# Interleaved rotary embedding on one core: sin products in free row places, whole-row VectorE instructions, and four transfers taken apart

## The chip, the cores and the metric

The kernel runs on one core of a Trainium2 chip. The metric is device time in microseconds of one execution, here the median of three runs. VectorE, GpSimd and 16 DMA engines do the work; ScalarE and SyncE issue one transfer each, TensorE has nothing to do.

## The reference

`x` is (8, 2048, 16, 64) in fp32: batch, sequence position, head, head dimension. `cos` and `sin` are (2048, 32). Neighbouring elements of the head dimension form pairs that are rotated by the angle of their position:

```
x1, x2 = x[..., 0::2], x[..., 1::2]
out[..., 0::2] = x1 * cos - x2 * sin
out[..., 1::2] = x1 * sin + x2 * cos
```

`cos` and `sin` hold for all batches and heads of a position. The output is fp32, of the shape of `x`.

## The kernel before, in words

The 2048 positions are split over 128 partitions, 16 positions (`K = 16`) to a partition, so that one batch element is one "row": 16 sub-rows of 1024 elements in each partition. A row is 8 MB in DRAM and 4 MB in SBUF, where it lies as bf16: the transfers of GpSimd's queue cast on the way in and on the way out. SBUF holds six row places (`buf`, shown as the tile `xt`); `at = [0, 1, 2, 3, 4, 5, 0, 1]` says which place row b uses, so rows 6 and 7 take the places of rows 0 and 1.

For each group of sub-rows `rotate` issues three VectorE instructions: the product with the sin table into `qt` (line 78), the product with the cos table in place (line 84), and the sum of the row with the pairs of `qt` exchanged (line 90). The sin table holds (sin, -sin) in turn, the cos table every value twice. Before, `qt` is one small buffer of its own of four sub-rows (`KP = 4`), and `rotate_row` goes through a row in four such groups, 12 instructions to a row.

The order is written out by hand (`tc.manual_schedule`); each engine works its own instructions in that order, with semaphores between them where data or places are shared.

- Start: ScalarE's queue loads the first four sub-rows of row 0 as fp32 into place 5, where `cos` and `sin` arrive as well; GpSimd's queue issues load(0) (the other 12 sub-rows), cos, sin, load(1) and load(2, 2), which is rows 2 and 3 in one transfer. VectorE casts the first sub-rows (line 107) and makes both tables (lines 109 to 114). Then place 5 is free and GpSimd issues load(4, 2).
- Middle: VectorE rotates rows 0 to 3. GpSimd waits to issue store(0, 2): in row 3's second group, after the first `GATE` sub-rows of the sin product, VectorE copies one element of place 0 onto itself (line 83, the gate), and the store waits for that copy. store(2, 2) follows when row 3 is done, then load(6, 2), which waits until stores 0 and 1 have landed, then store(4, 2) after row 5.
- End: store(6), then store(7) of 12 sub-rows. Before the last four sub-rows VectorE copies one element into row 6's place (line 140), and so waits until store(6) has landed; their sum goes as fp32 into place 3, and SyncE's queue stores it (line 142).

Transfers of GpSimd's queue are worked in the order of issue. `load` issues at line 56, `store` at line 59.

Of the kernel before, what the change touches and what calls it, by code (L numbers as in the profile page):

```python
# [2 lines left out]

# [4 lines left out]


@with_exitstack  # L10
def kernel(
    ctx: ExitStack,
    tc: tile.TileContext,
    x: bass.AP,
    cos: bass.AP,
    sin: bass.AP,
    out: bass.AP,
):
    nc = tc.nc
    fp32 = mybir.dt.float32  # L20
    bf16 = mybir.dt.bfloat16
    mult = mybir.AluOpType.mult
    add = mybir.AluOpType.add

    B, S, H, D = x.shape
    P = 128
    K = S // P
    D2 = D // 2
    HD = H * D
    NX = 6  # L30
    KP = 4
    HEAD = 4
    TAIL = 4
    GATE = 1

    x_t = x.rearrange("b (p k) h d -> p b k (h d)", p=P, k=K)
    out_t = out.rearrange("b (p k) h d -> p b k (h d)", p=P, k=K)
    cos_t = cos.rearrange("(p k) c -> p (k c)", p=P, k=K)
    sin_t = sin.rearrange("(p k) c -> p (k c)", p=P, k=K)

    consts = ctx.enter_context(tc.tile_pool(name="consts", bufs=1))
    rows_pool = ctx.enter_context(tc.tile_pool(name="rows", bufs=1))
    stage = ctx.enter_context(tc.tile_pool(name="stage", bufs=1))

    c_tab = consts.tile([P, K, D], bf16)
    s_tab = consts.tile([P, K, D], bf16)


    buf = rows_pool.tile([P, NX, K, HD], bf16, name="xt")
    at = [0, 1, 2, 3, 4, 5, 0, 1]  # L50

    def place(b, n=1, k0=0, k1=K):
        return buf[:, at[b] : at[b] + n, k0:k1]

    def load(b, n=1, k0=0, k1=K):
        nc.gpsimd.dma_start(out=place(b, n, k0, k1), in_=x_t[:, b : b + n, k0:k1])  # L56

    def store(b, n=1, k0=0, k1=K):
        nc.gpsimd.dma_start(out=out_t[:, b : b + n, k0:k1], in_=place(b, n, k0, k1))  # L59

    def rotate(b, k0=0, k1=K, gate=None, to=None):
        nk = k1 - k0
        xp = buf[:, at[b], k0:k1]
        qt = stage.tile([P, KP, HD], bf16, name="qt", tag="work")

        def rows(a):
            return a.rearrange("p k (h e) -> p k h e", h=H, e=D)

        def tab(a, j0=0, j1=nk):
            return dataclasses.replace(  # L70
                a,
                offset=a.offset + (k0 + j0) * D,
                ap=[a.ap[0], [D, j1 - j0], [0, H], [1, D]],
            )


        for a, z in ((0, nk),) if gate is None else ((0, GATE), (GATE, nk)):
            nc.vector.tensor_tensor(  # L78
                out=rows(qt[:, a:z]), in0=rows(xp[:, a:z]), in1=tab(s_tab, a, z), op=mult
            )  # L80
            if z < nk:
                one = buf[:1, at[gate], 0, :1]
                nc.vector.tensor_copy(out=one, in_=one)  # L83
        nc.vector.tensor_tensor(out=rows(xp), in0=rows(xp), in1=tab(c_tab), op=mult)  # L84
        q_swap = dataclasses.replace(
            qt, offset=qt.offset + 1, ap=[qt.ap[0], [2, nk * HD // 2], [-1, 2]]
        )
        x3 = xp.rearrange("p k (a j) -> p (k a) j", j=2)
        y3 = x3 if to is None else to.rearrange("p k (a j) -> p (k a) j", j=2)
        nc.vector.tensor_tensor(out=y3, in0=x3, in1=q_swap, op=add)  # L90

    with tc.manual_schedule():

        def fp32_in(b, k0, k1):
            return buf[:, at[b], k0:k1].rearrange("p k e -> p (k e)").bitcast(fp32)

        head = fp32_in(5, 0, 2 * HEAD).rearrange("p (k e) -> p k e", e=HD)
        cos_sb = fp32_in(5, K - 2, K - 1)
        sin_sb = fp32_in(5, K - 1, K)
        nc.scalar.dma_start(out=head, in_=x_t[:, 0, :HEAD])  # L100
        load(0, k0=HEAD)
        nc.gpsimd.dma_start(out=cos_sb, in_=cos_t)  # L102
        nc.gpsimd.dma_start(out=sin_sb, in_=sin_t)  # L103
        load(1)
        load(2, 2)

        nc.vector.tensor_copy(out=buf[:, at[0], :HEAD], in_=head)  # L107
        s2 = s_tab.rearrange("p k (i j) -> p (k i) j", j=2)
        nc.vector.tensor_copy(out=s2[:, :, 0], in_=sin_sb)  # L109
        nc.vector.tensor_scalar_mul(s2[:, :, 1], sin_sb, -1.0)  # L110
        nc.vector.tensor_copy(  # L111
            out=c_tab.rearrange("p k (i j) -> p (k i) j", j=2),
            in_=cos_sb.to_broadcast([P, K * D2, 2]),
        )

        load(4, 2)

        def rotate_row(b, k1=K, gate=None):
            for k in range(0, k1, KP):
                rotate(b, k, k + KP, gate if k == KP else None)  # L120

        rotate_row(0)
        rotate_row(1)
        rotate_row(2)
        rotate_row(3, gate=0)
        store(0, 2)
        store(2, 2)
        load(6, 2)
        rotate_row(4)
        rotate_row(5)  # L130
        store(4, 2)
        rotate_row(6)
        store(6)
        rotate_row(7, K - TAIL)
        store(7, k1=K - TAIL)

        tail = fp32_in(3, 0, 2 * TAIL).rearrange("p (k e) -> p k e", e=HD)
        nc.vector.tensor_copy(out=buf[:1, at[6], 0, :1], in_=buf[:1, at[7], K - 1, :1])  # L140
        rotate(7, K - TAIL, K, to=tail)
        nc.sync.dma_start(out=out_t[:, 7, K - TAIL :], in_=tail)


# [1 line left out]
_INS = ['x', 'cos', 'sin']  # L146
_OUTS = [((8, 2048, 16, 64), 'float32')]


# [23 lines left out]
```

## Time and profile before

| what | value |
|---|---|
| median of 3 runs | 316.95 us (316.95 to 317.0) |
| the profiled execution: own time, span | 316.72 us, 314.9 us |
| VectorE busy | 225.9 us (72%), 103 instructions |
| GpSimd busy | 7.9 us (2%), 16 instructions |
| HBM read, written | 67.63 MB, 67.11 MB |
| packets' time on GpSimd's queue (q0), share of 16 engines | 96.6% |

The profile is of one execution. Its span goes from the first to the last instruction; 1.8 us of the execution's time lie outside it. The page shows the span in 40 slices of 7.87 us. Its GB/s count what is written: 200 in a slice of loads (bf16) and 400 in a slice of stores (fp32) are the same traffic on the DRAM side. A group's row gives line, engine, operation, shapes and count, then busy time and the mean ns of one instruction, then the idle time ahead of it and what ended that. A row of a window gives its two ends, its length, the busy time of VectorE (DVE) and GpSimd (POOL) with instruction counts, the granted clock of TensorE, the DMA engines' busy share and GB/s.

### The profile page before, as it was taken

To read this page: it belongs to the slowest core of one execution; us is meant where nothing else is said; L and a number is where in the kernel's file an instruction comes from. 1 tells how busy PE (TensorE), PEld (TensorE's weight loads), DVE (VectorE), ACT (ScalarE), POOL (GpSimd) and SP (SyncE) were. 2 spreads that over 40 slices of the span, in tenths; PEclk is the share of its full clock that TensorE was granted. 3 is DMA by queue.
4 is the path that set the end of the run, shared out by engine and by line. 5 is a ranking of instruction groups with operands and counts; after the bars stand their busy time and mean duration, and the time that the engine had idled before them with its cause. 6 is when DMAs were issued, how large, how long until landed. Compare 5 with 4: busy or idle time off the path is not lost.

```text
span 314.9 us, 176 instructions
## 1 busy us (share of the span) xinstructions
DVE 225.9 (72%) x103; POOL 7.9 (2%) x16
## 2 busy tenths in 40 slices
DVE  0029999999899999999999995000009999992550
POOL 4000000000000000000000000000000000000000
DMA  7999999999999999999999999999999999999996
GB/s 255 261 283 200 200 208 258 200 200 221 246 200 200 246 221 400 400 516 417 400 400 524 408 400 400 262 204 200 204 320 408 400 449 474 408 400 483 425 424 266
DMA packets 2658, 102.25 MB, mean 325 GB/s; under 512 B 225, under 2 KB 225, under 8 KB 353
## 3 DMA queue, kind: packets, MB, share of 16 engines
q0 software_dynamic: 2368, 98.04, 96.6%
q10 hardware_dynamic: 144, 2.10, 1.8%
q1 hardware_dynamic: 144, 2.10, 1.6%
q14 instruction: 2, 0.01, 0.0%
HBM read 67.63 MB, written 67.11 MB: 428 GB/s over the span
## 4 chain that ended last, share of the span: by engine, by line
DVE 65%; DMA 16%; another core or an unknown queue 14%; issue 1%; POOL 0%; DVEq 0%; PEldq 0%
DVE xt L90 22%; DVE xt L84 21%; DVE qt L78 21%; DMA out_dram<-xt 9%; DMA xt<-in_sin_dram 7%; POOL xt L56 0%; DVE c_tab L111 0%; POOL xt L102 0%; DVE s_tab L109 0%; DVE s_tab L110 0%; DVE xt L140 0%; DVE xt L83 0%; DVEq L78 0%; PEldq L168 0%
## 5 line engine op out<-in xcount | busy, mean ns | idle before, releaser
L78 DVE TENSOR_TENSOR qt<-xt,s_tab 128x4096 bf16<-128x4096 bf16 (+2 forms) x33 | 73.4, 2226 | 45.1 <-DMA xt<-in_x_dram 44.2
L90 DVE TENSOR_TENSOR xt<-xt,qt 128x4096 bf16<-128x4096 bf16 (+1 forms) x32 | 75.5, 2359 | 1.1
L84 DVE TENSOR_TENSOR xt<-xt,c_tab 128x4096 bf16<-128x4096 bf16 x32 | 73.4, 2292 | 1.1
L107 DVE CAST xt<-xt 128x4096 bf16<-128x4096 f32 x1 | 2.3, 2294 | 15.3 <-DMA xt<-in_x_dram 15.3
L59 POOL DMA_DIRECT2D out_dram<-xt x5 | 3.2, 644 | 235.1 <-DVE xt L90 143.6
L140 DVE COPY xt<-xt 1x1 bf16<-1x1 bf16 x1 | 0.1, 144 | 9.1 <-DMA out_dram<-xt 9.1
L109 DVE CAST s_tab<-xt 128x512 bf16<-128x512 f32 x1 | 0.5, 452 | 6.3 <-DMA xt<-in_sin_dram 6.3
L56 POOL DMA_DIRECT2D xt<-in_x_dram x5 | 3.4, 683 | 43.3 <-DMA out_dram<-xt 21.3
L111 DVE CAST c_tab<-xt 128x1024 bf16<-128x1024 f32 x1 | 0.7, 684 | 0.0
L103 POOL DMA_DIRECT2D xt<-in_sin_dram x1 | 0.6, 562 | 0.0
L102 POOL DMA_DIRECT2D xt<-in_cos_dram x1 | 0.6, 554 | 0.0
L110 DVE TENSOR_SCALAR s_tab<-xt 128x512 bf16<-128x512 f32 x1 | 0.4, 442 | 0.0
L83 DVE COPY xt<-xt 1x1 bf16<-1x1 bf16 x1 | 0.1, 136 | 0.0
L157 POOL MEMSET const-float32-0.0<- 128x1 f32 x1 | 0.1, 98 | 0.2 <-issue 0.2
L157 POOL MEMSET const-bfloat16-1.0<- 128x1 bf16 x1 | 0.1, 101 | 0.0
L157 POOL MEMSET const-float32-1.0<- 128x1 f32 x1 | 0.1, 98 | 0.0
L157 POOL MEMSET const-uint8-127<- 128x1 uint8 x1 | 0.1, 98 | 0.0
## 6 DMA issues: line engine op xcount, KB each, us to landing
xt<-in_x_dram POOLq DMA_DIRECT2D x3, 8192.0 KB, 78.2
out_dram<-xt POOLq DMA_DIRECT2D x1, 6144.0 KB, 23.3
xt<-in_x_dram POOLq DMA_DIRECT2D x1, 4096.0 KB, 40.1
xt<-in_x_dram POOLq DMA_DIRECT2D x1, 3072.0 KB, 21.3
xt<-in_x_dram ACTq DMA_DIRECT2D x1, 2048.0 KB, 14.6
out_dram<-xt SPq DMA_DIRECT2D x1, 2048.0 KB, 10.2
xt<-in_cos_dram POOLq DMA_DIRECT2D x1, 256.0 KB, 21.3
xt<-in_sin_dram POOLq DMA_DIRECT2D x1, 256.0 KB, 21.4
```

The source lines that it names most:

```text
L56: nc.gpsimd.dma_start(out=place(b, n, k0, k1), in_=x_t[:, b : b + n, k0:k1])
L59: nc.gpsimd.dma_start(out=out_t[:, b : b + n, k0:k1], in_=place(b, n, k0, k1))
L78: nc.vector.tensor_tensor(out=rows(qt[:, a:z]), in0=rows(xp[:, a:z]), in1=tab(s_tab, a, z), op=mult)
L84: nc.vector.tensor_tensor(out=rows(xp), in0=rows(xp), in1=tab(c_tab), op=mult)
L90: nc.vector.tensor_tensor(out=y3, in0=x3, in1=q_swap, op=add)
L102: nc.gpsimd.dma_start(out=cos_sb, in_=cos_t)
L103: nc.gpsimd.dma_start(out=sin_sb, in_=sin_t)
L107: nc.vector.tensor_copy(out=buf[:, at[0], :HEAD], in_=head)
L109: nc.vector.tensor_copy(out=s2[:, :, 0], in_=sin_sb)
L110: nc.vector.tensor_scalar_mul(s2[:, :, 1], sin_sb, -1.0)
L111: nc.vector.tensor_copy(out=c_tab.rearrange("p k (i j) -> p (k i) j", j=2), in_=cos_sb.to_broadcast([P, K * D2, 2]),)
L157: nc = _bacc.Bacc("TRN2", target_bir_lowering=False, num_devices=1)
```

## The change

The buffer for the sin products shrinks in use: `rotate` gets `via`, the number of a row place that is free at that time, and writes its products there; without `via` it uses the small buffer, now allocated once. With `via` most rows are done whole:

- rows 0 and 1 whole, through place 4; load(4) is issued after row 1, so it waits for that row's last sum;
- the first half of row 2 in one group of eight sub-rows, through place 5; load(5) is issued after it; the rest of row 2 and all of row 3 stay in groups of four;
- the gate in row 3 stands after two sub-rows instead of one; store(0) and store(1) are issued one by one;
- rows 4 and 5 whole, through place 0, so row 4 waits until store(0) has landed; load(6, 2) comes after them and waits for row 5's last sum;
- row 6 whole and the first 12 sub-rows of row 7 in one group, through place 2; the last four through place 2 too.

GpSimd instead of VectorE makes the sin table, ahead of load(4) in its queue. VectorE has 61 instructions instead of 117 (waits and the like counted).

```diff
-    GATE = 1
+    GATE = 2
...
+    small = stage.tile([P, KP, HD], bf16, name="qt")
...
-    def rotate(b, k0=0, k1=K, gate=None, to=None):
+    def rotate(b, k0=0, k1=K, gate=None, to=None, via=None):
         nk = k1 - k0
         xp = buf[:, at[b], k0:k1]
-        qt = stage.tile([P, KP, HD], bf16, name="qt", tag="work")
+
+        qt = small if via is None else buf[:, via]
...
-        nc.vector.tensor_copy(out=s2[:, :, 0], in_=sin_sb)
-        nc.vector.tensor_scalar_mul(s2[:, :, 1], sin_sb, -1.0)
+        nc.gpsimd.tensor_copy(out=s2[:, :, 0], in_=sin_sb)
+        nc.gpsimd.tensor_scalar_mul(s2[:, :, 1], sin_sb, -1.0)
         nc.vector.tensor_copy(
             out=c_tab.rearrange("p k (i j) -> p (k i) j", j=2),
             in_=cos_sb.to_broadcast([P, K * D2, 2]),
         )
 
-        load(4, 2)
-
-        def rotate_row(b, k1=K, gate=None):
-            for k in range(0, k1, KP):
-                rotate(b, k, k + KP, gate if k == KP else None)
-
-        rotate_row(0)
-        rotate_row(1)
-        rotate_row(2)
-        rotate_row(3, gate=0)
-        store(0, 2)
+        rotate(0, via=at[4])
+        rotate(1, via=at[4])
+        load(4)
+        rotate(2, 0, K // 2, via=at[5])
+        load(5)
+        for k in range(K // 2, K, KP):
+            rotate(2, k, k + KP)
+        for k in range(0, K, KP):
+            rotate(3, k, k + KP, gate=0 if k == KP else None)
+        store(0)
+        store(1)
         store(2, 2)
+        rotate(4, via=at[0])
+        rotate(5, via=at[0])
         load(6, 2)
-        rotate_row(4)
-        rotate_row(5)
         store(4, 2)
-        rotate_row(6)
+        rotate(6, via=at[2])
         store(6)
-        rotate_row(7, K - TAIL)
+        rotate(7, 0, K - TAIL, via=at[2])
         store(7, k1=K - TAIL)
...
-        rotate(7, K - TAIL, K, to=tail)
+        rotate(7, K - TAIL, K, to=tail, via=at[2])
```

## The prediction

> **What bounds the kernel now.** I read the slices first.
>
> ```profile
> DMA  7999999999999999999999999999999999999996
> ```
>
> The 16 DMA engines are busy in every slice but the first and the last. VectorE (72%) has holes, the transfers have none. To see whether "9" hides gaps I asked for short windows at the turns of the queue; a packet counts where it starts, and GB/s times the window gives the bytes.
>
> ```profile
> 80.90:81.45 0.55, 0.04 (x1) 0.00 (x0) 1.00 4.46 953
> 117.20:117.70 0.50, 0.50 (x3) 0.00 (x0) 1.00 4.91 1049
> 119.70:120.20 0.50, 0.50 (x1) 0.00 (x0) 1.00 4.91 2097
> ...
> 141.30:141.90 0.60, 0.60 (x1) 0.00 (x0) 1.00 4.08 1748
> 143.80:144.40 0.60, 0.60 (x1) 0.00 (x0) 1.00 4.15 1761
> 146.20:146.70 0.50, 0.50 (x1) 0.00 (x0) 1.00 4.59 1966
> 147.10:147.20 0.10, 0.10 (x1) 0.00 (x0) 1.00 1.53 655
> ...
> 312.24:312.70 0.46, 0.00 (x0) 0.00 (x0) 1.00 1.33 570
> ...
> 313.10:313.20 0.10, 0.00 (x0) 0.00 (x0) 1.00 0.40 164
> ```
>
> 1049 x 0.5 = 524 KB are the last 16 load packets of rows 4 and 5 (32 KB each as written, 64 KB as read); 2097 x 0.5 = 1049 KB are the first 16 store packets, 2.48 us later. The beat is 2.42 us everywhere, eight beats (19.3 us) to a row, so the turn from loads to stores cost under 0.1 us. The end is set by bytes. A change can win only what makes an engine late, and loses what starves the queue.
>
> One engine is late. At 143.80:144.40 there are 1761 x 0.6 = 1057 KB: 16 packets of 65.5 KB and 8 KB more. One beat on, 146.20:146.70 holds 983 KB, 15 packets, and the 16th comes by itself at 147.1. That engine stays late: at the end all 16 start a packet in 312.24:312.70 (262 KB, 16 x 16.4), and one more starts alone at 313.14. The page has the 8 KB:
>
> ```profile
> q14 instruction: 2, 0.01, 0.0%
> ```
>
> It is a fetch of program. At 144.05 the trace lists VectorE at the 63rd of its instructions, waits and drains counted; no other engine has more than 34. In the trace's records of landings, 15 engines report the tail landed by 313.61 and the late one at 314.09. So 0.48 us of the span is this fetch.
>
> Next, who issues what (GpSimd's own timeline) and VectorE's chain:
>
> ```profile
> 25.52 0.72 POOL L56 DMA_DIRECT2D xt<-in_x_dram  x1 [21.27 <-DVE c_tab L111]
> 117.75 0.70 POOL L59 DMA_DIRECT2D out_dram<-xt  x1 [91.50 <-DVE xt L83]
> ```
>
> ```profile
> 2.44 21.40 DMA xt<-in_sin_dram
> ...
> 78.65 2.29 DVE xt L90
> 80.94 0.77 another core or an unknown queue
> ...
> 193.56 43.21 another core or an unknown queue
> ```
>
> Loads 4 and 5 were issued at 25.52, 55 us early; stores 0 and 1 at 117.75, 1.95 us before the packets of 119.70; load(6, 2) at 160.02, as stores 0 and 1 had landed. VectorE ends rows 0 and 1 at 80.94 and waits 0.77 for rows 2 and 3; it ends row 5 at 193.56 and waits 43 us for rows 6 and 7.
>
> **VectorE's instructions.** The groups, shapes apart:
>
> ```profile
> L84 DVE TENSOR_TENSOR xt<-xt,c_tab 128x4096 bf16<-128x4096 bf16 x32 | 73.4, 2292 | 1.1
> L78 DVE TENSOR_TENSOR qt<-xt,s_tab 128x1024 bf16<-128x1024 bf16 x1 | 0.7, 693 | 0.0
> L109 DVE CAST s_tab<-xt 128x512 bf16<-128x512 f32 x1 | 0.5, 452 | 6.3 <-DMA xt<-in_sin_dram 6.3
> ```
>
> (2292-693)/3072 = 0.5205 ns an element. A whole row (16384) is 2292 + 12288 x 0.5205 = 8688 ns, half a row 4424; from start to start add 34 ns (2326 between starts against 2292). A row costs 3 x 8.72 = 26.17 us instead of 12 x 2.326 = 27.92. VectorE's busy time falls from 225.9 to about 217. No transfer waits for that: worth nothing by itself.
>
> **The table of sin on GpSimd.** sin lands at 23.84. GpSimd starts 0.3 after its releaser (117.45 to 117.75), so at 24.14. No GpSimd arithmetic stands in the trace. From below the pair costs what VectorE paid, 0.89 us; as c_tab then lies beside it, the first product could even come 0.1 earlier than 25.14. From above I take four times VectorE, 3.6. I choose twice, 1.8: GpSimd's only wide work, the DMA issues, costs 0.54 to 0.76 apiece. The first product then starts at 26.0. The Trainium skill, "GPSIMD Engine Reference", section 3.1, gives 769 ns for 512 elements of a tight loop; by that the pair is an estimated 1.54 us and the start 25.8. No row here shows it.
>
> **Load 4 waits for rotate(1).** Its place holds the products of rows 0 and 1. 26.0 + 2 x 26.17 = 78.3, GpSimd at 78.6. Its first packets are due at 80.95. For stores 0 and 1 a start 1.95 before the due time was early enough; here it is 2.3, 0.35 to spare, so the pair may cost 2.15. Nothing else is queued on GpSimd then. What is beyond that stops all 16 engines and, as no gap follows that could take it up, is paid in full.
>
> **Load 5** waits for half of row 2: 81.81 + 3 x 4.46 = 95.2, due at 100.3. **The gate**: half a row in large products saves 0.59 and GATE=2 adds 0.53 (1024 elements), so it opens at 117.4 instead of 117.45 and store 0 starts on time. Store 1's issue, some 0.7, runs while store 0 moves. The two further ends of transfers are a 4-byte packet per engine each, 0.02 and 0.04 us in the records: +0.06.
>
> **Row 4 waits for store 0**, whose place takes its products. VectorE ends row 3 at 137.2; store 0 lands about 139.9 (119.9 + 8 x 2.42 + 0.6): 2.7 idle. Behind that wait stand rows 4 and 5, and behind them load(6, 2) on GpSimd: 139.9 + 52.3 = 192.2, issue at 192.5 instead of 160.02, due at 196.95, so 4.4 before, where 1.95 is enough. store(4, 2) is behind it, due at 235.9. Rows 6 and 7 end at 262.5 and, 12 sub-rows, 282.3; their stores are due at 274 and 293. The last chain (copy, three operations of 4 sub-rows, the SyncE store) keeps its shapes; its packets start after store(7)'s at 308, 4 us after their issue at 303.9.
>
> **The fetch.** 61 instructions end before the 63rd, where the fetch came; the late engine isn't late: -0.48.
>
> Sum on the profiled execution: span 314.9 - 0.48 + 0.06 = 314.5, own time 316.72 to 316.3. The median of the runs is 0.23 above that execution: 316.5, or -0.14%. A measurement of this kernel can tell about 0.2% (0.63 us) from no change, so this counts as the same.
>
> **The rivals.**
> - *The fetch stays.* The count that sets it off may include what the trace doesn't list. Then 316.95 + 0.06 = 317.0. For it: one fetch alone shows no rule. The Trainium skill, "Runtime: NRT & Kernel Launch", section Instruction fetch mechanics, has refills in blocks of 256 instructions, by which neither 117 nor 61 would cross one; the 8 KB packet in mid-program speaks against that reading, and a result of 317.0 hangs on it.
> - *Load 4 is late (slower).* It decides from a pair of 2.15 us. At 3.6 the gap is 1.45 and the time 317.9; at 2.8 it is 317.1. For it: the spare is 0.35 and GpSimd's price is unseen. Against: its queue is empty and VectorE idle at that moment, and 1.95 is only the shortest lead shown, not the least needed.
> - *Load(6, 2) is late (slower).* Spare 2.4 over six whole-row products, 0.4 each: 9.12 instead of 8.72. If one cost four small ones, 9.31, the gap is 1.1 and the time 317.6. Against: the straight line from 1024 to 4096.
> - *The late engine cost more than 0.48 (faster by over 0.2%).* It started some 0.6 to 0.7 behind at 147.1; with 0.66 of that back the time is 316.35, and with 0.15 of the scatter between executions (0.23 separates the profiled one from the median) 316.2. Against: the last of the other 15 engines lands only 0.48 earlier.
>
> **How the numbers follow.** Forecast 0.49 (of it 0.06 below 316.3, counted faster); fetch stays 0.10; load 4 late 0.18 (0.14 of it beyond 317.6, the rest within 0.2%); load(6, 2) late 0.06, all slower; larger gain 0.14; slower by something I don't name 0.03. Faster 0.06 + 0.14 = 0.20; slower 0.14 + 0.06 + 0.03 = 0.23; same 0.43 + 0.10 + 0.04 = 0.57. Range 316.2 to 317.9: the larger gain below, the dear pair above; about 0.15 is left out.
>
> **What would show it.** Queue 14 without its 8 KB packet and all engines' last packets together within 312.2 to 313.3; GpSimd's pair near 0.9 us each; load 4 issued near 78.6 with packets at 81.0; VectorE idle some 2.7 before row 4; load(6, 2) issued near 192.5; VectorE near 217 busy. A window without packets longer than 2.5 us near 81 or 197 would prove me wrong, and so would the 8 KB packet anywhere before 308.

## The result, and the profile after

The changed kernel takes 320.54 us in the median (316.84 to 321.4, 9 runs) against 316.72 us before (316.5 to 317.0, 9 runs): 1.1% slower, ratio 1.011, interval 1.0078 to 1.0143. I had forecast 316.5, with a range up to 317.9. The profiled execution took 321.0 us with a span of 319.0, 4.1 above the span before. Its times scatter over 4.6 us where those of before keep within 0.5; one of its nine runs took 316.84, so now and then an execution loses almost nothing.

Where the time is can't be seen in the slices, which still show full DMA engines:

```profile
DVE  0026999998799999919999995000007999990560
DMA  8999999999999999999999999999999999999995
```

The share counts a packet as busy for as long as it is open, whether it moves bytes or waits. So I took the windows again, and worked out from each row a second number: share x length x 16 engines / packets is how long a packet was open, and load packets are GB/s x length / 32.8 KB. After, at the start of load 4, at the turn to store 0, at the turn to store 4 and at the end:

```profile
80.90:81.45 0.55, 0.00 (x0) 0.00 (x0) 1.00 3.29 655
81.45:82.80 1.35, 1.12 (x1) 0.00 (x0) 1.00 0.70 121
117.50:118.75 1.25, 1.22 (x2) 1.02 (x2) 1.00 2.45 393
234.80:237.25 2.45, 0.00 (x0) 0.00 (x0) 1.00 1.15 201
312.70:313.20 0.50, 0.00 (x0) 0.00 (x0) 1.00 1.16 492
```

Before, all 16 first packets of rows 4 and 5 started in 80.90:81.45 (953 x 0.55 = 524 KB). Now 11 do (360 KB) and 5 come later (163 KB), and the 16 together are open 2.75 us each instead of 2.45. The last load packets ahead of the stores are open 2.45 x 1.25 x 16 / 15 = 3.27 us at 118 and 1.15 x 2.45 x 16 / 15 = 3.0 us at 235; before, those at 118 were open 2.45 (4.91 x 0.5 in the row of 117.20:117.70). In 312.70:313.20, where before a single packet of 16.4 KB started, 246 KB do. Queue 14 doesn't stand in the page's list of queues any more: the 8 KB fetch is gone from the span.

GpSimd's timeline has the issues, and the list of waits has row 4's wait for store 0:

```profile
23.87 0.75 POOL L112 CAST s_tab<-xt 128x512 bf16<-128x512 f32 x1 [19.61 <-DMA xt<-in_sin_dram]
24.66 1.64 POOL L113 TENSOR_SCALAR s_tab<-xt 128x512 bf16<-128x512 f32 x1
78.95 0.61 POOL L58 DMA_DIRECT2D xt<-in_x_dram  x1 [52.65 <-DVE xt L93]
117.44 1.07 POOL L61 DMA_DIRECT2D out_dram<-xt  x2 [21.36 <-DVE xt L86]
196.14 0.72 POOL L58 DMA_DIRECT2D xt<-in_x_dram  x1 [58.24 <-DVE xt L93]
```

```profile
DVE xt L81 <- DMA out_dram<-xt: 6.6, 1, 6.6
```

Store 0 is issued at 117.44, in time; load 4 at 78.95 instead of 78.6, which leaves it a lead of 2.0 us before its first packets are due at 80.95; load(6, 2) comes at 196.1 instead of 192.5, because row 4 waited 6.6 us and not 2.7.

The trace keeps each packet's start and duration, but not its engine. Followed engine by engine (the next packet is taken to be the one that starts where the last ended), the time beyond the 2.41 us beat was, in microseconds:

| stage | mean of 16 engines | the engine that ended last |
|---|---|---|
| start of load 4, 81 | 0.79 | 2.72 |
| turn from loads to store 0, 118 | 0.98 | 1.38 |
| start of load(6, 2), 198 | 0.55 | 0.05 |
| turn from loads to store 4, 235 | 0.61 | 0.98 |

Before, none of the four is above 0.1 in the mean. The last engine's four add up to 5.1. The span is 4.6 above that of a version without these losses (the first experiment); the rest is that this engine was not the last of the 16 when it began to lose.

At 198 only the eight engines that were due first lose time, 0.4 to 1.6 us. The other eight start their first packet 2.5 us or more after the issue, and those packets are open as short as ever (7 of them in this row, 0.54 x 2 x 16 / 7 = 2.47 us):

```profile
198.60:200.60 2.00, 0.00 (x0) 0.00 (x0) 1.00 0.54 115
```

At 235 all 16 lose 0.3 to 1.0, these eight too; the engine that ended last is one of them.

### The profile page after: what moved, and what is told of

Same layout as the page of the kernel before. It is cut to its first block, busy times and chain, and to the rows that moved or that the text cites. A ratio compares the mean times of both kernels' runs of the same rounds, so it can differ in the third digit from the quotient of the medians.

```text
span 319.0 us, 128 instructions
## 1 busy us (share of the span) xinstructions
DVE 216.7 (68%) x47; POOL 11.1 (3%) x20
## 4 chain that ended last, share of the span: by engine, by line
DMA 45%; DVE 38%; issue 11%; POOL 1%; another core or an unknown queue 1%; POOLq 0%; DVEq 0%; PEldq 0%
DMA out_dram<-xt 24%; DMA xt<-in_x_dram 14%; DVE xt L93 13%; DVE xt L87 12%; DVE xt L81 10%; DMA xt<-in_sin_dram 7%; DVE qt L81 3%; POOL s_tab L113 1%; POOL s_tab L112 0%; POOL xt L58 0%; POOL xt L105 0%; POOL out_dram L61 0%; DVE xt L143 0%; DVE xt L86 0%
## 5 line engine op out<-in xcount | busy, mean ns | idle before, releaser
L81 DVE TENSOR_TENSOR xt<-xt,s_tab 128x16384 bf16<-128x16384 bf16 (+3 forms) x8 | 56.7, 7089 | 57.3 <-DMA xt<-in_x_dram 48.1
L87 DVE TENSOR_TENSOR xt<-xt,c_tab 128x4096 bf16<-128x4096 bf16 (+3 forms) x14 | 70.5, 5035 | 0.5
L93 DVE TENSOR_TENSOR xt<-xt 128x16384 bf16<-128x16384 bf16 (+3 forms) x8 | 58.9, 7359 | 0.3
L81 DVE TENSOR_TENSOR qt<-xt,s_tab 128x4096 bf16<-128x4096 bf16 (+1 forms) x7 | 13.9, 1983 | 0.2
L93 DVE TENSOR_TENSOR xt<-xt,qt 128x4096 bf16<-128x4096 bf16 x6 | 13.8, 2292 | 0.2
L113 POOL TENSOR_SCALAR s_tab<-xt 128x512 bf16<-128x512 f32 x1 | 1.6, 1638 | 0.0
L112 POOL CAST s_tab<-xt 128x512 bf16<-128x512 f32 x1 | 0.8, 752 | 19.6 <-DMA xt<-in_sin_dram 19.6
```

The costliest lines, as they stand in the source:

```text
L81: nc.vector.tensor_tensor(out=rows(qt[:, a:z]), in0=rows(xp[:, a:z]), in1=tab(s_tab, a, z), op=mult)
L112: nc.gpsimd.tensor_copy(out=s2[:, :, 0], in_=sin_sb)
L113: nc.gpsimd.tensor_scalar_mul(s2[:, :, 1], sin_sb, -1.0)
```

## The experiments

Three explanations were tested. Theory A: load 4 was issued too late for some engines, and each late load is paid twice, at its start and at the next turn from loads to stores (the second loss). Theory B: the transfers taken apart cost. Theory C: whole-row instructions slow the packets beside them.

**Loads 4 and 5 early.** Row 1's products go through place 5, so that load 4 is issued after row 0 and load 5 after row 1. All else of the change stays but the large group of row 2.

```diff
         rotate(0, via=at[4])
-        rotate(1, via=at[4])
         load(4)
-        rotate(2, 0, K // 2, via=at[5])
+        rotate(1, via=at[5])
         load(5)
-        for k in range(K // 2, K, KP):
+        for k in range(0, K, KP):
             rotate(2, k, k + KP)
```

> The changed kernel, but load 4 is issued after row 0 (its products alone use place 4) and load 5 after row 1, whose products use place 5; row 2 is done in four groups. So loads 4 and 5 are issued at about 52.8 and 79, 28 and 21 us before their packets are due. All else as changed: one transfer each for rows 4, 5, 0, 1, whole rows, rows 4 and 5 through place 0, load(6, 2) after them. Theory A (late issue: in the changed kernel load 4's packets start up to 1.6 us late on some engines, the engines fall out of step, and an engine out of step loses again at each turn from loads to stores): no gap near 81, all engines' last load packets near 117.5 take 2.43 us, row 4 starts near 140, load(6, 2) is issued near 192.5; 316.4 to 317.2. Theory B (the transfers taken apart and the stores issued 0.3 us earlier): the turn at 118 still costs 0.5 to 1.4, time 318 to 320. Theory C (whole-row instructions of VectorE slow the packets beside them): 319 to 321.

Measured: 316.33 us (316.09 to 317.18), ratio to before 0.9993 (0.9984 to 1.0003), span 314.4, where my sum had been 314.5. Its windows are as even as those of before:

```profile
80.90:81.45 0.55, 0.00 (x0) 0.00 (x0) 1.00 4.46 953
...
196.80:197.40 0.60, 0.00 (x0) 0.00 (x0) 1.00 4.12 874
233.10:233.75 0.65, 0.00 (x0) 0.00 (x0) 1.00 2.81 605
...
312.65:313.20 0.55, 0.00 (x0) 0.00 (x0) 1.00 0.02 0
```

All 16 packets at 81; 4.12 x 0.6 x 16 / 16 = 2.47 us a packet at 197; 2.81 x 0.65 x 16 / 12 = 2.44 at the turn to stores; nothing left after 312.65. This kernel keeps whole rows, stores 0 and 1 apart and GpSimd's table, so B and C fall. Stores 0 and 1 were issued at 118.20, 1.4 us before their first packets, at 119.57, and none came late.

**No load within 20 us of being due.** Row 5's products go through place 1, load 6 is issued after row 4, load 7 after row 5.

```diff
         rotate(4, via=at[0])
-        rotate(5, via=at[0])
-        load(6, 2)
+        load(6)
+        rotate(5, via=at[1])
+        load(7)
```

> As the run before it, and row 5's products use place 1, so that load 6 is issued after row 4 (about 166.5, due 197) and load 7, now apart, after row 5 (192.5, due 216). No transfer is then issued within 20 us of being due but the first store. Theory A: 316.4 to 316.7, 0.0 to 0.5 below the run before it. Theories B and C: as the run before it, 318 to 321.

Measured: 316.4 us (316.14 to 317.04), ratio 0.9994 (0.9984 to 1.0003), span 314.4, the same as the run before it. The 4.4 us by which load(6, 2) is ahead there is enough.

**One late load in the kernel before.** Line 83's trick is used for load(4, 2): a one-element write into its places, made behind a chosen instruction of row 1's last group, holds it back.

```diff
-        load(4, 2)
...
         nc.vector.tensor_tensor(out=rows(xp), in0=rows(xp), in1=tab(c_tab), op=mult)
+        if late == 1:
+            nc.vector.memset(buf[:1, at[4]:at[4] + 2, 0, :1], 0.0)
...
-        rotate_row(1)
+        rotate_row(1, late=1)
+        load(4, 2)
```

> The kernel before, with one thing changed: load(4, 2), still one transfer, waits for a one-element write that VectorE makes behind the second-last instruction of row 1, so it is issued near 79.0, the time at which the changed kernel issues load 4, 1.95 us before its packets are due. Theory A: packets near 81 start 0 to 1.6 late, engines out of step, last load packets at 118 and 235 take 2.7 to 3.9 instead of 2.43, time 318.5 to 321. Theories B and C: 316.9 to 317.3. If only the gap itself counts and the turns are clean: 318.5.

> As the run before it, with the write one instruction earlier, so that load(4, 2) is issued near 76.6, 4.35 us before its packets are due. Theory A with the latest packet of the changed kernel (4.67 us from issue to its full pace): 316.9 to 317.4, engines nearly in step. If the needed lead is under 2 us, as my prediction took it, this and the run before it both give 316.9.

Measured with the issue at 78.95: 319.15 us (319.09 to 319.68), ratio 1.0081 (1.0066 to 1.0096). With the issue at 76.56: 316.58, ratio 0.9998 (0.9989 to 1.0007). The first one's windows, and the second one's at 81:

```profile
80.90:81.45 0.55, 0.06 (x1) 0.00 (x0) 1.00 3.53 715
81.45:82.40 0.95, 0.60 (x1) 0.00 (x0) 1.00 0.75 138
117.25:117.95 0.70, 0.70 (x3) 0.21 (x1) 1.00 2.19 468
117.95:119.15 1.20, 1.17 (x2) 0.49 (x1) 1.00 1.06 164
...
80.90:81.45 0.55, 0.00 (x0) 0.00 (x0) 1.00 4.46 953
```

In the first, 12 packets are on time and 4 late; in the second all 16 are on time. At the first one's turn the engines that were on time start 10 last packets of 2.19 x 0.7 x 16 / 10 = 2.45 us; the six that come after 117.95 are open 1.06 x 1.2 x 16 / 6 = 3.4. Engine by engine the second loss goes with the first: 1.9 us at 81 and 1.5 at 118 on the worst, nothing and nothing on six. So one late load alone, in an otherwise untouched kernel, costs 2.5 us of the 3.8, and 2.4 us more of lead removes all of it. Nor is VectorE's work beside the issue the reason: after load 4's issue it is busy here until 80.95, while in the changed kernel it was idle from 78.65 to 81.68, and the load is late in both.

**The same, behind row 1's last instruction,** so that all engines run dry.

```diff
-        rotate_row(1, late=1)
+        rotate_row(1, late=2)
```

> The kernel before with load(4, 2) issued only behind row 1's last sum, near 81.3, 0.3 us after its packets are due, so that all 16 engines run dry. With packets 2.2 to 4.7 us behind the issue the engines start 2 to 4 late. Theory P with a second loss as large as the first on each engine (so it was within 0.4 on the engines of the run with load(4, 2) at 79): last load packets before the stores take 4 to 6 us, 320.5 to 323. If the second loss has a ceiling near 1.4, the largest seen on an engine so far: 320 to 321.5. If only the gap counts here: 319 to 320.5.

Measured: 319.96 us (319.7 to 320.24), ratio 1.0103 (1.0088 to 1.0118), with the issue at 81.14.

```profile
80.90:82.50 1.60, 0.48 (x1) 0.72 (x1) 1.00 0.01 0
82.50:83.20 0.70, 0.70 (x1) 0.00 (x0) 1.00 4.40 749
119.20:120.20 1.00, 0.96 (x2) 0.00 (x0) 1.00 3.26 524
```

No packet starts for 1.4 to 2.0 us after the issue, and the 16 first ones are open 4.40 x 0.7 = 3.08 us: with the 0.65 us beyond 2.43 added, an idle queue is at full pace an estimated 2.0 to 2.7 us after the issue. The Trainium skill, "DMA: Bandwidth & Descriptors", section Specifications, gives about 1 us to the first byte on GpSimd's path; counted here from the start of the issue instruction to a packet's start, it is more. The second loss (3.26 us a packet, 0.85 in the mean) is not as large as the first (2.1): my "as large as the first" was wrong, and no engine's second loss (0.6 to 1.1 here) is above 1.4. The time alone, just under the range for that case, would also fit a single loss; the row of 119.20 shows the second.

**GpSimd's table back on VectorE, in the changed kernel.**

```diff
-        nc.gpsimd.tensor_copy(out=s2[:, :, 0], in_=sin_sb)
-        nc.gpsimd.tensor_scalar_mul(s2[:, :, 1], sin_sb, -1.0)
+        nc.vector.tensor_copy(out=s2[:, :, 0], in_=sin_sb)
+        nc.vector.tensor_scalar_mul(s2[:, :, 1], sin_sb, -1.0)
```

> The changed kernel with the sin table made by VectorE again, as before. The first product then starts near 25.2 instead of 26.3, row 1 ends 1.1 us sooner and load 4 is issued near 77.8, 3.1 us before it is due. Theory A with a needed lead between 1.95 (late by up to 1.6) and 4.35 (not late): if packets reach their pace 2.2 to 4.7 us after the issue, as in the changed kernel, a few engines are still up to 0.5 late, 316.5 to 318.5; if the needed lead is under 3 us, in step, 316.3 to 316.7. Theory that GpSimd's slow table has nothing to do with it: 320 to 321 as the changed kernel.

Measured: 317.4 us (316.64 to 319.84), ratio 1.0028 (1.001 to 1.0046). Load 4 is issued at 77.86, 3.1 before it is due. In its profile (318.5 us, slower than the median) three engines lose 0.3 to 1.1 at 81. Only the one that lost 1.1 loses again at 118 (0.35). Load(6, 2) is issued 3.3 us before it is due:

```profile
196.90:198.70 1.80, 0.00 (x0) 0.00 (x0) 1.00 1.38 291
234.70:235.00 0.30, 0.00 (x0) 0.00 (x0) 1.00 0.64 109
```

Its 16 first packets are open 1.38 x 1.8 x 16 / 16 = 2.48 us, as in the first experiment (2.47), so none waited; the last of them starts at 198.6, because its engine brought its lateness along. At 235 that engine alone loses again: its last load packet, the one in the second row, is open 0.64 x 0.3 x 16 = 3.07 us. So GpSimd's table costs 3.1 us of the 3.8, and it does so through the leads of the loads: the first experiment keeps that table and loses nothing.

**Only load(6, 2) late.** The first experiment's kernel with an idle product of five sub-rows behind row 5.

```diff
         rotate(5, via=at[0])
+        nc.vector.tensor_tensor(
+            out=buf[:, at[6], :5], in0=buf[:, at[5], :5], in1=buf[:, at[4], :5], op=mult
+        )
         load(6, 2)
```

> The first of my runs (loads 4 and 5 early) with an idle product of five sub-rows of VectorE written into place 0 after row 5; it adds 2.85 us ahead of load(6, 2), which is then issued near 195.3 instead of 192.4, 1.6 us before its packets are due, with all engines in step. Theory A: first packets near 198 late by 0.4 to 2.5, engines out of step; 317.5 to 319 if the turn to stores at 235 then costs again, 317 to 318 if it doesn't. If only load 4's place in the order matters: 316.4.

Measured: 318.65 us (318.1 to 319.11), ratio 1.0057 (1.0042 to 1.0073), with the issue at 195.25.

```profile
196.80:197.40 0.60, 0.00 (x0) 0.00 (x0) 1.00 5.30 874
233.40:235.60 2.20, 0.00 (x0) 0.00 (x0) 1.00 1.58 238
```

The first packets are open 5.30 x 0.6 = 3.2 us instead of 2.47, the last ones 1.58 x 2.2 = 3.5 instead of 2.44. All 16 engines lose 0.3 to 1.4 at 198 and 0.6 to 1.4 at 235, and the second loss isn't larger where the first was. Being out of step alone isn't what makes it, as I had put it in the first expectation. In the run with load(4, 2) at 78.95 the engines are still some 3 us apart at 235, behind a load(6, 2) issued at 162.28, and nothing is lost there (16 packets, 0.94 x 2.6 x 16 / 16 = 2.44 us each):

```profile
233.00:235.60 2.60, 0.00 (x0) 0.00 (x0) 1.00 0.94 202
```

**The stores behind it issued later.** Two one-element copies hold store(4, 2) until stores 2 and 3 have landed.

```diff
+        for p in (2, 4):
+            one = buf[:1, at[p], 0, :1]
+            nc.vector.tensor_copy(out=one, in_=one)
         store(4, 2)
```

> The run with load(6, 2) issued near 195.3, and store(4, 2) made to wait until stores 2 and 3 have landed, so that it is issued near 199 instead of 195.96, after the late loads have begun and 38 us before its own turn. In the run with load(6, 2) late the last load packets ahead of store(4, 2) took 3.0 to 3.8 us instead of 2.43, a second loss of about 1.1 an engine. Theory P (the second loss belongs to loads that were issued late, whenever the stores behind them are issued): it stays, 318 to 319. Theory Q (it comes from stores queued in the same moment as the late loads): the last load packets take 2.43, 317.3 to 317.7.

Measured: 318.8 us (318.61 to 318.9), ratio 1.0067 (1.005 to 1.0084); the store is issued at 198.19 and the last load packets are open 3.3 us. The second loss stays, so Theory Q falls.

**The transfers apart in the kernel before.**

```diff
-        load(4, 2)
+        load(4)
+        load(5)
...
-        store(0, 2)
+        store(0)
+        store(1)
```

> The kernel before with load(4, 2) as load 4 and load 5, and store(0, 2) as store 0 and store 1, issued back to back at the old times. Theory A and my sum (two more 4-byte packets per engine, 0.06): 316.6 to 316.8, turn at 118 to 120 clean. Theory B (the transfers taken apart cost): 318 or more.

Measured: 316.84 us (316.48 to 317.37), ratio 1.0003 (0.9994 to 1.0012), span 315.1: nothing beyond noise.

**The fetch of program.** The first experiment's kernel with rows 6 and 7 in groups of four.

```diff
-        rotate(6, via=at[2])
+        for k in range(0, K, KP):
+            rotate(6, k, k + KP)
...
-        rotate(7, 0, K - TAIL, via=at[2])
+        for k in range(0, K - TAIL, KP):
+            rotate(7, k, k + KP)
```

> The first of my runs (loads 4 and 5 early) with rows 6 and 7 in groups of four sub-rows: 15 more VectorE instructions, 77 in all of the kind that the trace lists, and no transfer issued late. If the 8 KB fetch of program comes with VectorE's 63rd instruction, it is back near row 6 or 7 (240 to 290 us), one engine ends 0.4 to 0.7 behind the others, and the span is 0.4 to 0.5 above the 314.4 of that run: 316.7 to 316.9. If the fetch does not hang on the count, 314.4 and 316.4.

Measured: 316.81 us (316.56 to 317.17), ratio to before 1.0002 (0.9994 to 1.0011), where the kernel without the 15 instructions has 0.9993. By time alone the two can't be told apart. The fetch is back, at 272.2, with VectorE at the 63rd instruction that the trace lists, as before:

```profile
q14 instruction: 1, 0.01, 0.0%
```

```profile
271.90:272.60 0.70, 0.70 (x1) 0.00 (x0) 1.00 3.56 1510
274.20:274.90 0.70, 0.70 (x1) 0.00 (x0) 1.00 3.31 1404
```

1510 x 0.7 = 1057 KB are 16 packets and 8 KB; a beat later 15 come on time (983 KB). The last tail packet lands at 314.41, the other engines' by 313.82. The span is 0.8 above the 314.4; 0.6 of it is this engine, and 0.2 was lost by all engines alike near 100 us, which this experiment's edit doesn't explain. The four runs that edit only the transfers of the kernel before have the fetch too, at 142.2 to 144.2, with VectorE at its 63rd or 64th listed instruction; the kernels in which VectorE has 59 to 65 in all have none within the span.

**The version without a late load, over more rounds.** Same kernel as the second.

> The version without any late load (loads 4, 5, 6 and 7 each issued 16 us or more before their packets are due), measured over more rounds than before. Theory A with the fetch of program gone (0.48 us for one engine) and two to three more 4-byte packets per engine: 0.3 to 0.45 us below the kernel before, a ratio of 0.9986 to 0.999. If the fetch doesn't count: 1.000.

Measured: 316.21 us (316.07 to 316.4, 11 runs) against 316.59 (316.45 to 316.82), ratio 0.9988 (0.9979 to 0.9997). It is 0.38 us below the kernel before, just clear of noise; the first measurement of the same kernel (up to 1.0003) was not.

## Why the prediction was wrong

**The step that failed** is in "Load 4 waits for rotate(1)": "For stores 0 and 1 a start 1.95 before the due time was early enough; here it is 2.3, 0.35 to spare." The lead of a store at a turn was carried over to a load. The actual lead was 2.0, as good as the bound, and by the rule nothing should have been lost; 4 to 5 engines of 16 were late. At that place a load was on time with 4.35 and late on three engines with 3.1, while a store at the turn was on time with 1.4.

**The price of it** was too low: "paid in full" is paid nearly twice where it is worst. The kernel before with this one load late loses 1.9 us at its start and 1.5 at the turn to stores on its worst engine. My own range ended at 317.9 because I counted the gap once.

**What hung on it.** The late engine landed store 0 at 143.4 instead of 139.9, row 4 started 3.5 us later, and load(6, 2), with "4.4 before, where 1.95 is enough", was left with 1.8 before the earliest engines were due. It became a second late load, with its own turn at 235. I had taken the two rivals as separate cases; the first brings the second.

**GpSimd's pair** was mis-sized: 2.43 us from 23.87 to 26.30 where I chose 1.8. The cast (0.75) agrees with the 769 ns of the Trainium skill, "GPSIMD Engine Reference", section 3.1; the multiplication took 1.64, twice that. As GpSimd started 0.06 and not 0.3 after sin landed, the first product began only 0.3 later than I had it. The two errors nearly cancelled, which was luck: the pair was 0.28 over the deciding point of 2.15, the early start gave 0.24 of it back, and by the rule of 1.95 load 4 was still on time. So the rival "load 4 is late" named the right load, but by its own condition it would have cost nothing here.

**What held.** Whole-row instructions 8692 ns (8688), VectorE busy 216.7 us (217), load 4 issued at 78.95 (78.6), load 5 at 95.56, the gate open at 117.15 (117.4) and store 0 issued in time behind it, the fetch gone from the span. The whole sum for the span, 314.5, is met by the first experiment at 314.4. Its two small terms fit the runs: 0.48 for the fetch, where the version without a late load gains 0.38 in all, and 0.06 for the transfers taken apart, where the run with that edit alone shows nothing beyond noise. The last sign of being wrong is written the wrong way round: by the prediction's own sum the packets near 81 and 197 should have been open no longer than 2.5 us, and those at 81 were open 2.75.

**What stays open** is why a late load is paid again at the turn to the stores, 37 us after its first packet. In the changed kernel the packets that pay at 118 are load 5's, which was issued 4.7 us ahead; load 4's own last packets, at 98 to 100, are open 2.48 us at most. The second loss is 0.3 to 1.5 us large and stays when the stores behind it are issued 2.2 us later. It doesn't follow the late engines one by one in every run: at 235 in the changed kernel eight engines pay that had started load(6, 2) on time, and with the table back on VectorE two engines that were late at 81 don't pay at 118. No run without a late load has it. No run tested a mechanism.

## What to carry to other kernels

In a kernel whose DMA engines never rest, look up for every transfer the time between its issue and its packets' turn, before and after the edit: a wait that fits "just in time" must be judged by a transfer of the same direction and place in the order. Here 1.4 us were enough for a store and 3.1 were not for a load; whether the direction is the reason was not tested. A place reused as scratch moves a load's issue to the end of the work that uses it; spread the scratch over the places in the order in which they are refilled (row 0's products in place 4, row 1's in place 5) and the same instruction saving is free. The busy share doesn't show a starved engine: divide it by the packets.

## What the runs showed of the hardware

- A load issued to an idle queue of GpSimd: first packets 1.4 to 2.0 us after the issue, full pace after 2.0 to 2.7. With the queue running, a lead of 1.95 left 4 of 16 engines with packets that started late and more that were open too long, 3.1 left three late, 4.35 none. At another turn, after stores, a load with 3.3 had none late. A store was on time with 1.4.
- The second loss at the turn from late loads to stores: 0.85 us a packet in the mean with all engines dry, up to 1.5 on one engine; its cause is open.
- An 8 KB fetch of program came with VectorE's 63rd or 64th listed instruction, at 142.2 to 144.2 us in the kernel before and four variants of it and at 272.2 in the kernel with 15 more instructions. In the two traces that were followed to the end one DMA engine then landed 0.5 to 0.6 us behind the others (314.09 against 313.61, 314.41 against 313.82).
